# Forgetting attention in a hybrid decoder layer: who subtracts the weights' low parts, how two column minima are compared, and when two factor rows are fetched

## The chip, the cores and the metric

The kernel runs on one core of a Trainium2 chip. The metric is the device time of one launch in microseconds (us); of several runs the median is taken, and lower is better.

A core has five engines that work side by side, each with its own queue of instructions that it takes in order: TensorE (PE in the profile; its weight loads are listed apart as PEld), VectorE (DVE), ScalarE (ACT), GpSimd (POOL) and SyncE (SP, which here only issues DMAs). Engines wait for each other by semaphores.

## The reference

One decoder layer in fp32 over 1024 tokens of width 1024, cut here to what matters:

```python
h = rmsnorm(x, ln1)
ml_qk, ml_v, ml_o, ml_i, ml_f, fx_q, fx_k, fx_v, fx_f = split(h @ w_in)
# 4 mLSTM heads of 128, 8 forgetting heads of 64
mh = mlstm_chunkwise(mq, mk, mv, ig, lf)
mh = mh * rsqrt(mean(mh * mh, -1) + EPS) * ml_norm          # per token and head
ml_out = mh * sigmoid(ml_o)
s  = fq @ fk.T * 64**-0.5 + (c[q] - c[k])                   # c: running sum of log forget gates
p  = softmax(where(q >= k, s, -inf))
fx_out = p @ fv
x = x + concat([ml_out, fx_out]) @ w_out
x = x + cross_attention(rmsnorm(x, ln_x), rmsnorm(mem, ln_mem), w_xq, w_xkv, w_xo)   # 256 memory tokens
u = relu(rmsnorm(x, ln2) @ w_ff1)
out = rmsnorm(x + (u * u) @ w_ff2, ln_f)
```

## The kernel before

**Split products.** A fp32 product is made of three matmuls. Every operand is split into a high part (a copy rounded to the type fp32r) and a low part (the operand less its high part); lines 186, 187 and 188 multiply low by high, high by low and high by high into one PSUM bank. For weights, a DMA brings the raw tile (`wr`, 2 buffers), ACT writes the high part (`wh`, 3 buffers) and a subtraction gives the low part (`wl`, 3 buffers). Outside the stretch that the change concerns, this is `split` (lines 132 and 133, or 135 and 136 with a scale): ACT, then DVE.

**The order.** The kernel is written in a tile framework, which orders each engine's instructions from a timeline of its own. In regions marked `in_order()` the order on PE, ACT, DVE and POOL is the written one; the DMA queue of SP is still ordered by the framework.

**Closing an mLSTM head** (`ml_head`, from line 611). The factors of 1024 tokens stand in 8 columns of `fac`. `to_row` turns them into a row: 128x8 are transposed on PE, copied by ACT, stored by DMA to a row of `facd` in DRAM, and read back, broadcast to all 128 partitions, for the first half of the tokens (512). The second half is read by a DMA of its own (line 623). Each half is multiplied into the head's result (lines 626 and 627), split, and stored to `mix` in DRAM. Both rows use the buffer tag "a" (`r_a` in the trace), which has one buffer, so the second row's read waits until the first row has been used. The last head (`hd == MLH - 1`) is closed while the forgetting attention has begun.

**Forgetting attention.** For each of 8 heads, 8 row tiles of 128 queries: tile i sees the first (i + 1) x 128 keys, in one part (i < 4) or two. A `Tile` goes through `score` (two matmuls, lines 736 and 737, and a triangular mask, line 716), `top` (DVE's negated maximum of a part, line 743; after the second part the lower of the two columns, line 746), `exp` (ACT, line 749, with the sum along the row; line 751 for the correction between the parts) and `scale` (DVE's reciprocal, lines 756 and 757; POOL scales the weights, line 760). The columns (`c_mx`, `c_den`) have 3 buffers each. A `Values` step transposes 128 keys' weights of four tiles on PE (`turn`, line 775), splits them (`cut`: ACT line 132, DVE line 133, into `r_d` and `r_e`, or into one larger buffer in every third step) and multiplies by the values into bank `ov` (`add`, line 795). There is one `ov` bank: `fx_close` (ACT line 804, DVE line 805 into `r_f`) empties it before the next half head starts.

**Slots.** `slot()` runs one step of each in a fixed order: `fx_close` if a half head has ended, `turn`, the adds of two slots ago, `top`, `cut`, `exp`, `scale` of the slot before, the next score part, then filler, then one half of a weight split. 13 slots run scores alone first; then the product by `w_fv` (`token_major`, plain weight loads at line 174 and splits by `split`) stands between, in which the last mLSTM head is closed; then slots run with values. Per head there are 12 score parts and 12 value steps.

**Filler.** PE's spare time in the slots is filled with other products: the keys and values of cross attention (16 weight tiles of 1024 columns) and the first part of the output product (16 weight tiles of 640 columns, `out_unit`; results added at line 932). Each of these 32 weight tiles is loaded by `raw_load` (line 950) and split in two halves, one at the end of a slot, by `cut_half`:

```python
hi, lo = cuts_[sources[n][0]][-1]
c = slice(e * c // 2, (e + 1) * c // 2)
s.activation(hi[:, c], raw[:, c], AF.Copy)
(v if e else g).tensor_tensor(out=lo[:, c], in0=raw[:, c], in1=hi[:, c].bitcast(F32), op=ALU.subtract)
halves[0] += 1
if e:
    raw_load()
```

So POOL subtracts the first half (e = 0) and DVE the second; the load that follows a second half waits until the raw tile is free again.

Of the kernel before, what the change touches and what calls it, by code (L numbers as in the profile page):

```python
# [9 lines left out]
F32 = mybir.dt.float32  # L10
F32R = mybir.dt.float32r
AF = mybir.ActivationFunctionType
ALU = mybir.AluOpType
# [4 lines left out]
P = 128  # L18
T = 1024
TH = 512  # L20
# [3 lines left out]
MLH = 4  # L24
# [20 lines left out]
def hybrid_layer(ctx: ExitStack, tc: tile.TileContext, a: dict, out: bass.AP):  # L45
    nc = tc.nc
    v, s, g = nc.vector, nc.scalar, nc.gpsimd
# [11 lines left out]
    def sb(tag, shape, bufs, dt=F32):  # L59
        return pool.tile(shape, dt, tag=tag, name=name(tag), bufs=bufs)  # L60

    def act(dt=F32R):
        return sb("act", [P, 8, TH], 7, dt)
# [15 lines left out]
    def w2(tag, n=512, dt=F32, p=P):  # L79
        return sb("r_" + tag, [P, 512], BUFS[tag], dt)[:p, :n]  # L80

    def col(tag, n=1, bufs=3):
        return sb("c_" + tag, [P, 8], bufs)[:, :n]
# [6 lines left out]
    def sc():  # L90
        return ps_tile("sc")
# [4 lines left out]
    def ov_():  # L96
        return ps_tile("ov")
# [13 lines left out]
    load = nc.sync.dma_start  # L111
# [17 lines left out]
    def split(hi, lo, src, scale=None):  # L129

        if scale is None:
            s.activation(hi, src, AF.Copy)  # L132
            return v.tensor_tensor(out=lo, in0=src, in1=hi.bitcast(F32), op=ALU.subtract)  # L133
        else:
            s.activation(hi, src, AF.Copy, scale=scale)
            return v.scalar_tensor_tensor(out=lo, in0=src, scalar=scale, in1=hi.bitcast(F32), op0=ALU.mult, op1=ALU.subtract)
# [47 lines left out]
    def mm3(ps, w, x, first, last, more=False):  # L184

        nc.tensor.matmul(ps, w[1], x[0], start=first, stop=False, skip_group_check=more)  # L186
        nc.tensor.matmul(ps, w[0], x[1], start=False, stop=False, skip_group_check=more)  # L187
        nc.tensor.matmul(ps, w[0], x[0], start=False, stop=last, skip_group_check=more)  # L188

    def both(pair, f):  # L190
        return f(pair[0]), f(pair[1])
# [24 lines left out]
    def rsqrt_cols(*args):  # L216
        rsqrt_guess(*args)()
# [6 lines left out]
    def sum_cols(ps, src, n):  # L224
        for t in range(n):
            nc.tensor.matmul(ps[:, t : t + 1], src[:, t * P : (t + 1) * P], ones, start=True, stop=True)
# [21 lines left out]
    def to_row(dst, cols, n, at, bank=None):  # L248

        ps = (bank or ov_)()  # L250
        nc.tensor.transpose(ps[:n, :P], cols, ident)
        s.activation(dst[:n, :P], ps[:n, :P], AF.Copy)
        load(at.rearrange("o (t q) -> (o t) q", t=n), dst[:n, :P])
        w = min(dst.shape[1], n * P)
        return load(dst, at[:, :w].broadcast_to([P, w]))
# [14 lines left out]
    at = 0  # L270
# [39 lines left out]
    def mv_of(hd, t):  # L310

        return mv[hd // 2][:, t, hd % 2 * 256 : hd % 2 * 256 + 256]
# [15 lines left out]
    for k in range(KT):  # L328
        if k % 2 == 0:
            c = slice(k % 4 * 256, k % 4 * 256 + 512)  # L330
# [44 lines left out]
    z, e, q, lf = (small[:, i:j].rearrange("p (t c) -> p t c", c=c) for i, j, c in ((0, 128, GC), (128, 224, GW), (224, 320, GW), (320, 416, GW)))  # L375
# [188 lines left out]
    facd = dram.tile([MLH, T], F32, name="facd")  # L564

    def ml_head(hd, q, k, og, num1, den1):
        fac = col("fac", 8)
        nums = []
        dens = col("dens", 8)
        sqs = col("sqs", 8)  # L570
        for hf in range(2):
            nmb = w2("a")
            load(nmb, rows[hd : hd + 1, hf * TH : hf * TH + TH].broadcast_to([P, TH]))
            num = ov_()
            acc = den1 if hf else w2("b")
            last = 4 * hf + 3
            for j in range(4 * hf, last + 1):
                d0 = j - 4 * hf
                c0 = min(d0 * P, 256)
                sp = sc()  # L580
                ks = both(k, lambda z: z[:, j * P : (j + 1) * P])
                mm3(sp[:, c0:], ks, both(q, lambda z: z[:, hf * TH + c0 : hf * TH + TH]), True, True)
                wt = acc if j == 0 else w2("c")
                s.activation(wt[:, c0:], nmb[:, c0:], AF.Exp, bias=gcol[:, j, hd : hd + 1])
                n_ = d0 * P + P - c0
                g.affine_select(out=wt[:, c0 : c0 + n_], in_=wt[:, c0 : c0 + n_], pattern=[[1, n_]], compare_op=ALU.is_ge, fill=0.0, base=c0 - d0 * P, channel_multiplier=-1)
                v.scalar_tensor_tensor(out=wt[:, c0:], in0=sp[:, c0:], scalar=float(P) ** -0.5, in1=wt[:, c0:], op0=ALU.mult, op1=ALU.mult)
                wh, wl = w2("d", dt=F32R), w2("e", dt=F32R)
                split(wh[:, c0:], wl[:, c0:], wt[:, c0:])
                if j:  # L590
                    g.tensor_tensor(out=acc[:, c0:], in0=wt[:, c0:], in1=acc[:, c0:], op=ALU.add)
                vj = mv_of(hd, j)
                mm3(num[:, c0:], (vj[:, :P], vj[:, P:]), (wh[:, c0:], wl[:, c0:]), d0 == 0, j == last)
            sq = w2("c")
            if hf:
                nsb = num1
                v.tensor_tensor(out=nsb, in0=num, in1=nsb, op=ALU.add)
                s.activation(sq, nsb, AF.Square)
            else:
                nsb = w2("f")  # L600
                s.activation(nsb, num, AF.Copy)
                s.activation(sq, num, AF.Square)
            ps = sc()
            sum_cols(ps[:, 0:4], acc, 4)
            sum_cols(ps[:, 4:8], sq, 4)
            s.activation(dens[:, 4 * hf : 4 * hf + 4], ps[:, 0:4], AF.Abs)
            v.tensor_copy(sqs[:, 4 * hf : 4 * hf + 4], ps[:, 4:8])
            nums.append(nsb)
        v.tensor_tensor(out=dens, in0=dens, in1=emc[:, :, hd], op=ALU.max)
        rd = col("rd", 8)  # L610
        v.reciprocal(rd, dens)
        v.tensor_tensor(out=sqs, in0=sqs, in1=rd, op=ALU.mult)
        v.tensor_tensor(out=sqs, in0=sqs, in1=rd, op=ALU.mult)
        rsqrt_cols(fac, sqs, 1.0 / P, 8)
        v.tensor_tensor(out=fac, in0=fac, in1=rd, op=ALU.mult)
        yield
        for hf in range(2):
            fb = w2("a")
            at = facd[hd : hd + 1]
            if hf == 0:  # L620
                to_row(fb, fac, 8, at, sc)
            else:
                load(fb, at[:, TH:].broadcast_to([P, TH]))
            yield
            y = nums[hf]
            v.scalar_tensor_tensor(out=y, in0=y, scalar=vec[:, VEC["ml_norm"] + hd : VEC["ml_norm"] + hd + 1], in1=fb, op0=ALU.mult, op1=ALU.mult)
            v.scalar_tensor_tensor(out=y, in0=og[:, hf * TH : hf * TH + TH], scalar=1.0, in1=y, op0=ALU.add, op1=ALU.mult)
            yh, yl = w2("y", dt=F32R), y.bitcast(F32R)
            split(yh, yl, y, 0.5)
            load(mix[hf, 0, :, hd], yh.bitcast(F32))  # L630
            load(mix[hf, 1, :, hd], yl.bitcast(F32))
# [86 lines left out]
    class Tile:  # L718
# [23 lines left out]
        def top(self, e):  # L742
            v.tensor_reduce(out=self.mxs[:, e : e + 1], in_=self.ps[e], axis=mybir.AxisListType.X, op=ALU.max, negate=True)
            if e:

                v.tensor_tensor(out=self.mxs[:, 1:2], in0=self.mxs[:, 0:1], in1=self.mxs[:, 1:2], op=ALU.min)

        def exp(self, e):
            s.activation(self.pt[:, slice(*self.parts[e])], self.ps[e], AF.Exp, bias=self.mxs[:, e : e + 1], accum_out=self.dens[:, e : e + 1])
# [195 lines left out]
    def raw_load():  # L945
        n = len(raws_)
        if n < len(sources):
            src = sources[n][1]
            raw = sb("wr", [P, 1024], 2)[:, : src.shape[-1]]
            last_raw[:] = [load(raw, src)]  # L950
            raws_.append(raw)

    def cut_half():

        n, e = divmod(halves[0], 2)
        raw = raws_[n]
        c = raw.shape[-1]
        if e == 0:
            cuts_.setdefault(sources[n][0], []).append(tuple(sb(t, [P, 1024], 3, F32R)[:, :c] for t in ("wh", "wl")))
        hi, lo = cuts_[sources[n][0]][-1]  # L960
        c = slice(e * c // 2, (e + 1) * c // 2)
        s.activation(hi[:, c], raw[:, c], AF.Copy)
        (v if e else g).tensor_tensor(out=lo[:, c], in0=raw[:, c], in1=hi[:, c].bitcast(F32), op=ALU.subtract)
        halves[0] += 1
        if e:
            raw_load()

    def cut_for(u, most=99):

        while most and halves[0] < 2 * len(sources) and sources[halves[0] // 2][0] <= u:  # L970
            cut_half()
            most -= 1
# [97 lines left out]
    for step in fill:  # L1070
        n, e = divmod(halves[0], 2)
# [8 lines left out]
    for hf in range(2):  # L1080
        hi, lo = act(), act()
# [623 lines left out]
```

## Time and profile before

| | before |
|---|---|
| median of 3 runs | 1520.9 us (1520.22 to 1521.38) |
| span of the profiled execution | 1518.6 us |
| that execution's own device time | not recorded apart from its span |
| granted TensorE clock, mean | 0.997 |
| PE idle in the span | 1518.6 - 1498.9 = 19.7 us |
| HBM traffic | 195 GB/s over the span |

The span runs from the first to the last instruction of one profiled execution; the device time of a run includes what lies around it. Busy times are per engine and overlap. A line number in the trace is that of the kernel before; `r_a` to `r_y` are buffers of the tags "a" to "y", `c_` are columns, `tp`, `sc`, `mm` and `ov` PSUM banks, `wr`, `wh` and `wl` the raw, high and low weights. The trace shows the work that is changed between about 370 and 590 us of the span.

### The profile page before, as it was taken

How to read it: one execution, taken by the hardware profiler on the slowest of the kernel's cores; microseconds unless marked ns; L12 is line 12 of the kernel's file. 1: busy time of each engine (PE TensorE's matmuls, PEld its weight loads, DVE VectorE, ACT ScalarE, POOL GpSimd, SP SyncE). 2: the span in 40 equal slices, each digit the busy share in tenths (PEclk: the TensorE clock that was granted, in tenths of full speed). 3: DMA queues.
4: the chain of work that ended last, by engine and by line, in shares of the span. 5: the costliest groups of instructions: out<-in, count | busy, mean ns of one | idle time of the engine just before them, and what ended most of it. 6: DMA issues, size and time to landing. Idle time of an engine off the chain costs nothing.

```text
span 1518.6 us, 21919 instructions
## 1 busy us (share of the span) xinstructions
PE 1498.9 (99%) x7697; PEld 1260.1 (83%) x7697; DVE 1100.2 (72%) x1744; ACT 723.7 (48%) x1349; POOL 436.9 (29%) x497
## 2 busy tenths in 40 slices
PE   8999999999999999999999999999999999999997
PEld 8988888889898888788888888888888888888887
DVE  7676675765798875854457887887887788777765
ACT  7333343334688763644343456565556332222124
POOL 1003030413455441001100033343344644333312
PEclk9999999999999999999999999999999999999998
DMA  6332333446887958953334436876775966555623
GB/s 240 89 107 87 113 104 127 131 130 164 267 252 225 291 195 281 321 195 119 122 135 155 164 123 232 281 276 239 271 256 217 360 260 222 222 222 215 255 85 111
DMA packets 118673, 298.28 MB, mean 196 GB/s; under 512 B 13202, under 2 KB 27852, under 8 KB 112420
## 3 DMA queue, kind: packets, MB, share of 16 engines
q1 hardware_dynamic: 118276, 296.79, 57.1%
q8 instruction: 60, 0.98, 0.3%
q14 instruction: 49, 0.40, 0.1%
q10 hardware_dynamic: 288, 0.11, 0.1%
HBM read 200.13 MB, written 96.72 MB: 195 GB/s over the span
## 4 chain that ended last, share of the span: by engine, by line
PE 92%; DMA 3%; DVE 2%; issue 1%; ACT 1%; POOLq 0%; SPq 0%; POOL 0%; DVEq 0%; ACTq 0%
PE tp L186 8%; PE tp L188 8%; PE tp L187 8%; PE sc L186 6%; PE sc L188 6%; PE sc L187 6%; PE m L186 6%; PE m L187 6%; PE m L188 6%; PE mm L186 6%; PE mm L187 6%; PE mm L188 6%; PE ov L186 2%; PE ov L187 2%; PE ov L188 2%; PE ov L795 2%
## 5 line engine op out<-in xcount | busy, mean ns | idle before, releaser
L186 PE MATMUL tp<-act,wl 128*128 128x512 f32 (+1 forms) x456 | 178.6, 392 | 0.0
L187 PE MATMUL tp<-act,wh 128*128 128x512 f32 (+1 forms) x456 | 178.5, 392 | 0.0
L188 PE MATMUL tp<-act,wh 128*128 128x512 f32 (+1 forms) x456 | 178.5, 392 | 0.0
L132 ACT ACTIVATE wh<-wr 128x1024 fp32r<-128x1024 f32 (+3 forms) x100 | 96.0, 961 | 116.4 <-PE tp L188 37.2
L133 DVE TENSOR_TENSOR wl<-wr,wh 128x1024 fp32r<-128x1024 f32 (+3 forms) x100 | 116.7, 1168 | 17.4 <-ACT wh L132 16.9
L186 PE MATMUL mm<-act,wl 128*128 128x512 f32 (+1 forms) x328 | 126.0, 384 | 0.5 <-DVE r_d L1091 0.5
L187 PE MATMUL mm<-act,wh 128*128 128x512 f32 (+1 forms) x328 | 125.8, 384 | 0.0
L188 PE MATMUL mm<-act,wh 128*128 128x512 f32 (+1 forms) x328 | 125.5, 383 | 0.0
L186 PE MATMUL m<-act,wl 128*128 128x512 f32 (+1 forms) x312 | 119.2, 382 | 0.8 <-DVE r_d L1091 0.8
L188 PE MATMUL m<-act,wh 128*128 128x512 f32 (+1 forms) x312 | 119.1, 382 | 0.0
L187 PE MATMUL m<-act,wh 128*128 128x512 f32 (+1 forms) x312 | 119.1, 382 | 0.0
L188 PEld LDWEIGHTS tp<-act,wh 128*128 128x128 f32 x456 | 85.7, 188 | 19.6
L186 PEld LDWEIGHTS tp<-act,wl 128*128 128x128 f32 x456 | 85.7, 188 | 19.1
L187 PEld LDWEIGHTS tp<-act,wh 128*128 128x128 f32 x456 | 85.8, 188 | 18.9
L186 PE MATMUL sc<-act,wl 128*128 128x512 f32 (+1 forms) x260 | 100.7, 387 | 0.0
L187 PE MATMUL sc<-act,wh 128*128 128x512 f32 (+1 forms) x260 | 100.5, 386 | 0.0
L188 PE MATMUL sc<-act,wh 128*128 128x512 f32 (+1 forms) x260 | 100.5, 386 | 0.0
L1439 POOL TENSOR_TENSOR z<-wr 128x256 f32<-128x256 f32 x56 | 52.7, 963 | 146.9 <-DMA wr<-w_ff2q 129.8
L132 ACT ACTIVATE w<-wr 128x768 fp32r<-128x768 f32 (+2 forms) x31 | 25.5, 825 | 131.2 <-PE tp L188 69.1
L132 ACT ACTIVATE wh<-z 128x1024 fp32r<-128x1024 f32 (+2 forms) x55 | 52.5, 956 | 65.0 <-POOL z L1439 29.8
L133 DVE TENSOR_TENSOR wl<-z,wh 128x1024 fp32r<-128x1024 f32 (+2 forms) x55 | 66.0, 1200 | 9.1 <-ACT wh L132 9.1
L188 PEld LDWEIGHTS mm<-act,wh 128*128 128x128 f32 x328 | 61.6, 188 | 12.9 <-issue 0.2
(656 smaller groups left out, 4189.6 us busy)
## 6 DMA issues: line engine op xcount, KB each, us to landing
act<-right SPq DMA_DIRECT2D x35, 1024.0 KB
right<-r_d SPq DMA_DIRECT2D x70, 256.0 KB
right<-w SPq DMA_DIRECT2D x56, 256.0 KB
wr<-w_ff2q SPq DMA_DIRECT2D x28, 512.0 KB
act<-fqk SPq DMA_DIRECT2D x48, 256.0 KB
wr<-w_in SPq DMA_DIRECT2D x20, 512.0 KB
wr<-w_ff SPq DMA_DIRECT2D x20, 512.0 KB
fqk<-r_p SPq DMA_DIRECT2D x32, 256.0 KB
```

What stands on the lines that cost most here:

```text
L132: s.activation(hi, src, AF.Copy)
L133: return v.tensor_tensor(out=lo, in0=src, in1=hi.bitcast(F32), op=ALU.subtract)
L186: nc.tensor.matmul(ps, w[1], x[0], start=first, stop=False, skip_group_check=more)
L187: nc.tensor.matmul(ps, w[0], x[1], start=False, stop=False, skip_group_check=more)
L188: nc.tensor.matmul(ps, w[0], x[0], start=False, stop=last, skip_group_check=more)
L795: nc.tensor.matmul(self.ov[:, c0:], self.fv[:, self.j], t[:, c0:], start=self.j == 0 and t is self.p[1], stop=self.last and t is self.p[0])
L1439: g.tensor_tensor(out=o, in0=x, in1=y, op=op)
```

## The change

Three edits. In `cut_half` the second half's subtraction is given to GpSimd as the first is. In `top` the lower of the two columns is found by an operation of one tensor with a per-partition scalar instead of one of two tensors. In `ml_head`, for the last head alone, the two rows get two buffers, "a" and "d"; both reads are issued right behind `to_row`'s store, and the high part of the second half's result goes to a buffer "e" instead of "y". For the other three heads the loads stay where they were (`hf != end` is true for `hf = 1` alone, and for the last head for `hf = 0` alone). Behind line 616 the new kernel's lines have numbers higher by 2. The numbers of instructions on each engine are unchanged but for the 32 subtractions that pass from DVE to POOL.

```diff
@@ ml_head
         yield
+        end = hd == MLH - 1
+        fbs = [w2("a"), w2("d")] if end else [None, None]
+        at = facd[hd : hd + 1]
         for hf in range(2):
-            fb = w2("a")
-            at = facd[hd : hd + 1]
+            fb = fbs[hf] or w2("a")
             if hf == 0:
                 to_row(fb, fac, 8, at, sc)
-            else:
-                load(fb, at[:, TH:].broadcast_to([P, TH]))
+            if hf != end:
+                load(fbs[1] or fb, at[:, TH:].broadcast_to([P, TH]))
             yield
...
-            yh, yl = w2("y", dt=F32R), y.bitcast(F32R)
+            yh, yl = w2("e" if end and hf else "y", dt=F32R), y.bitcast(F32R)
             split(yh, yl, y, 0.5)
@@ Tile.top
-                v.tensor_tensor(out=self.mxs[:, 1:2], in0=self.mxs[:, 0:1], in1=self.mxs[:, 1:2], op=ALU.min)
+                v.tensor_scalar(out=self.mxs[:, 1:2], in0=self.mxs[:, 1:2], scalar1=self.mxs[:, 0:1], scalar2=None, op0=ALU.min)
@@ cut_half
-        (v if e else g).tensor_tensor(out=lo[:, c], in0=raw[:, c], in1=hi[:, c].bitcast(F32), op=ALU.subtract)
+        g.tensor_tensor(out=lo[:, c], in0=raw[:, c], in1=hi[:, c].bitcast(F32), op=ALU.subtract)
```

## The prediction, made before the changed kernel was run

> **What bounds the kernel now.** I read the page first. TensorE (PE) is busy for almost the whole span:
>
> ```profile
> span 1518.6 us, 21919 instructions
> PE 1498.9 (99%) x7697; PEld 1260.1 (83%) x7697; DVE 1100.2 (72%) x1744; ACT 723.7 (48%) x1349; POOL 436.9 (29%) x497
> ```
>
> The timed runs have their median at 1520.9 us, 2.3 us above the span of the profiled execution; what lies around the span is not shown by itself, so I make the sum on the span and add it to the median as it stands. The runs lie between 1520.22 and 1521.38, and about 0.2% (3.0 us) is what a measurement of this kernel can tell from no change.
>
> All three edits act between 360 and 600 us, so next I asked for the busy times of that stretch alone:
>
> ```profile
> 360.00:600.00 240.00, 236.53 (x1587) 211.90 (x1586) 187.91 (x443) 163.16 (x438) 103.53 (x161) 1.00 0.79 246
> ```
>
> The columns after the length are PE, weight load, VectorE (DVE), ScalarE (ACT) and GpSimd (POOL). PE stands still for 240.00 - 236.53 = 3.47 us, and the clock is 1.00. So nothing that speeds another engine can return much more than these 3.47 us, while work made late can cost without such a ceiling. DVE, at 78%, is the busiest engine beside PE, POOL the idlest at 43%: the change moves work from the one to the other. The question is which of the 3.47 us of waits end on DVE.
>
> **The moved subtraction.** The groups of this stretch, kept apart by shape, give its price on either engine, and the price of the comparison (line 746):
>
> ```profile
> L963 POOL TENSOR_TENSOR wl<-wr,wh 128x512 fp32r<-128x512 f32 x16 | 21.4, 1340 | 5.1 <-ACT wh L962 3.8 <-issue 1.3
> ...
> L963 DVE TENSOR_TENSOR wl<-wr,wh 128x512 fp32r<-128x512 f32 x16 | 14.8, 923 | 1.2 <-ACT wh L962 1.1
> ...
> L963 POOL TENSOR_TENSOR wl<-wr,wh 128x320 fp32r<-128x320 f32 x16 | 14.0, 876 | 26.9 <-ACT wh L962 21.6 <-DVE r_p L932 2.7 <-DVE r_b L932 2.6
> ...
> L963 DVE TENSOR_TENSOR wl<-wr,wh 128x320 fp32r<-128x320 f32 x16 | 10.1, 631 | 1.1 <-ACT wh L962 1.0
> ...
> L746 DVE TENSOR_TENSOR c_mx<-c_mx 128x1 f32<-128x1 f32 x32 | 8.9, 279 | 1.1
> ```
>
> 32 second halves leave DVE: 14.8 + 10.1 = 24.9 us. POOL takes on 16 of 1.34 us and 16 of 0.876 us, 35.5 us at most. POOL goes to about 103.5 + 35.5 = 139 of 240 us (58%), DVE to about 163 (68%). Both have room on average. PE's matmuls are the same ones, so its own work does not change.
>
> Does DVE's relief reach PE? Here is the worst place, from the timeline of POOL, ACT, DVE and PE (start, length, engine, line, and in brackets the idle time before it):
>
> ```profile
> 489.59 1.45 POOL L963 TENSOR_TENSOR wl<-wr,wh 128x512 fp32r<-128x512 f32 x1
> ...
> 489.73 0.48 ACT L132 ACTIVATE r_d<-tp 128x384 fp32r<-128x384 f32 x1
> ...
> 489.86 1.73 DVE L963 TENSOR_TENSOR wl<-wr,wh 128x512 fp32r<-128x512 f32 x1
> ...
> 490.58 0.60 ACT L804 ACTIVATE r_c<-ov 64x512 f32<-64x512 f32 x1
> ...
> 491.56 0.28 PE L188 MATMUL mm<-wh,act 128*128 128x256 f32 x1
> ...
> 491.85 0.54 DVE L133 TENSOR_TENSOR r_e<-tp,r_d 128x384 fp32r<-128x384 f32 x1
> ...
> 492.45 0.33 PE L775 MATMUL tp<-ident,w 128*128 128x128 f32 x1 [0.61 <-DVE r_e L133]
> ...
> 492.75 0.69 DVE L805 TENSOR_TENSOR r_f<-ov,r_c 64x512 f32<-64x512 f32 x1
> ...
> 493.49 0.50 PE L795 MATMUL ov<-r_e,w 128*128 128x512 f32 x1 [0.66 <-DVE r_f L805]
> ```
>
> The reader is to see a DVE subtraction of 1.73 us that begins inside POOL's and ends after it. Behind it in DVE's queue stand the split of the transposed weights (491.85) and the sum that frees the output bank (492.75), and PE waits for both, 0.61 + 0.66 = 1.27 us. Without it the split has its input at 489.73 + 0.48 = 490.21 and the sum has its own at 490.58 + 0.60 = 491.18, each more than a microsecond before it now starts. Both waits should go. ACT's inputs are late next, and they are early enough for PE.
>
> A second such place, at the change from one head to the next:
>
> ```profile
> 426.53 0.59 ACT L804 ACTIVATE r_c<-ov 64x512 f32<-64x512 f32 x1
> ...
> 426.54 1.15 DVE L963 TENSOR_TENSOR wl<-wr,wh 128x512 fp32r<-128x512 f32 x1
> ...
> 427.72 0.68 DVE L805 TENSOR_TENSOR r_f<-ov,r_c 64x512 f32<-64x512 f32 x1
> ...
> 428.46 0.50 PE L795 MATMUL ov<-r_e,w 128*128 128x512 f32 x1 [0.44 <-DVE r_f L805]
> ```
>
> The sum could start when ACT is done, at 426.53 + 0.59 = 427.12 instead of 427.72. That is 0.60 us, more than the 0.44 us waited.
>
> **What holds POOL's added work.** Where POOL waits now, and what waits for the halves:
>
> ```profile
> POOL act L760 <- DVE c_den L757: 44.5, 22, 7.5
> ...
> POOL w L760 <- DVE c_den L757: 18.8, 14, 4.3
> ...
> SPq L950 <- DVE wl L963: 22.9, 14, 4.5
> ...
> ACT wh L962 <- DMA wr<-w_xv: 1.9, 1, 1.9
> ```
>
> POOL's scalings of the softmax weights (line 760) wait 44.5 + 18.8 = 63.3 us for DVE's reciprocals. A second half that runs in such a gap delays no scaling, and the 35.5 us would fit in it 1.8 times. Queued behind a second half on POOL are the next slot's scalings, for which ACT's exponentials and DVE's maxima wait three tiles later, through their three column buffers, and PE's transposes. Its own reader is PE's filler matmul. One of the tightest second halves:
>
> ```profile
> 407.77 0.68 DVE L963 TENSOR_TENSOR wl<-wr,wh 128x512 fp32r<-128x512 f32 x1
> ...
> 410.71 0.28 PE L187 MATMUL mm<-wl,act 128*128 128x256 f32 x1
> ```
>
> It ends 2.26 us before its use; 1.34 instead of 0.68 us takes 0.66 us of that, and a scaling ahead of it less than 1.6 more. This still fits, barely.
>
> The load of the next weights (line 950) stands on SP's queue behind the second half: 14 such waits now, 22.9 us. It is issued later by the same 0.66 us or more, and the loads of queries and keys behind it too. In the order of the changed program one to three of those loads have moved ahead of it at several places. ACT has waited for weight data for 1.9 us only, at one place, so mostly nothing is lost. I price this from 0 to 1.0 us (half of that 1.9 us once more) and take 0.4, nearer to no wait.
>
> **The comparison.** In the queries of lines 746 and 757 (lengths: least, median, most) and in the timeline:
>
> ```profile
> L746 DVE TENSOR_TENSOR c_mx<-c_mx x32: 151/160/1073, 375.8 to 558.3; 128x1 f32<-128x1 f32 x32
> ```
>
> ```profile
> L757 DVE RECIPROCAL c_den<-c_den x64: 144/156/167, 371.6 to 562.3; 128x1 f32<-128x1 f32 x64
> ```
>
> ```profile
> 400.96 1.30 POOL L963 TENSOR_TENSOR wl<-wr,wh 128x512 fp32r<-128x512 f32 x1
> ...
> 401.21 1.07 DVE L746 TENSOR_TENSOR c_mx<-c_mx 128x1 f32<-128x1 f32 x1
> ```
>
> A comparison of one column takes 1.07 us when it falls into a POOL subtraction, and ends with it (402.28 against 402.26). A reciprocal of one column, with one tensor input, has never taken over 0.167 us. The row that the new form resembles most is the reciprocal, since it reads one tensor and a scalar: 8.9 - 32 x 0.156 = 3.9 us of DVE time freed at best, nothing at worst. No PE wait above ends on line 746, so it adds nothing to the sum and only shortens DVE's queue.
>
> [...]
>
> **The two factor rows.** In the chain of waits, and then in the timeline:
>
> ```profile
> 373.10 4.12 DMA r_a<-facd
> ...
> 378.02 3.87 DMA r_a<-facd
> ```
>
> ```profile
> 381.92 0.75 DVE L626 SCALAR_TENSOR_TENSOR r_f<-r_f,vec,r_a 128x512 f32<-128x512 f32 x1 [2.00 <-DMA r_a<-facd]
> ...
> 382.77 0.47 ACT L749 ACTIVATE act<-sc,c_mx 128x256 f32<-128x256 f32 x1 [2.03 <-DVE c_mx L746]
> ...
> 383.39 0.50 PE L736 MATMUL sc<-act 128*128 128x512 f32 x1 [0.41 <-ACT act L749]
> ```
>
> The second row is fetched only after the first has been used, DVE waits 2.00 us for it with a comparison queued behind, ACT's exponential waits for that, and PE 0.41 us. With a buffer of its own the second load is issued right behind the first, near 373.5, and lands near 378. The three links shorten and the 0.41 us go. The other moved pieces (the two stores of the results and the five filler matmuls that now stand behind the row's transpose) have no reader close by: nothing. The borrowed buffers are needed again only at the first value tiles.
>
> **What stays.** Two waits at the change to the slots end on ACT's own order:
>
> ```profile
> 395.20 0.45 PE L736 MATMUL sc<-act 128*128 128x384 f32 x1 [0.72 <-ACT act L749]
> ...
> 399.01 0.38 PE L736 MATMUL sc<-act 128*128 128x256 f32 x1 [0.37 <-ACT w L749]
> ```
>
> The order of these instructions on ACT and PE is not changed, so 1.09 us remain.
>
> **Sum.** 1.27 + 0.44 + 0.41 = 2.12 us go by the bracketed idle times. They count short: between the starts at 491.56 and 492.45 lie 0.89 us, of which 0.28 count as busy, although such matmuls otherwise follow each other faster. With at most 0.2 us more for each of four waits the gain is between 2.1 and 2.9 us; I take 2.6. Less 0.4 for the later loads: 2.2 us. The span becomes 1516.4, the time 1520.9 - 2.2 = 1518.7 us.
>
> **Rivals.**
> (a) *All waits go.* A shorter DVE queue also removes the 1.09 us at the change and the rest: 3.47 + 6 x 0.2 = 4.7 us at most, 1516.5 us taken. For it: DVE is at 78%, and 29 us of its 188 may go. Against: those waits end on ACT. Chance 0.22; were the new comparison held up as the old one is, I would give it 0.12.
> (b) *It does nothing that shows.* PE has 99%, and ACT, at 163 of 240 us, takes DVE's place at the same points: only the row's 0.41 us are left, 1520.5 us. Against: both ACT inputs above are ready long before. Chance 0.15.
> (c) *POOL falls behind.* At each head's change tiles come one per slot instead of one per two, and POOL has a scaling and a subtraction in each. If a whole subtraction is late there, three tiles later maxima and exponentials wait and PE with them: 1.34 us in four of eight heads and 0.876 in four, 8.9 us, 1529 us with DVE's gain just lost; 1525 us if it is half of the heads. It decides when the gaps per head, 63.3 / 8 = 7.9 us, fall below the added 35.5 / 8 = 4.4 us. Against: they are nearly twice as long, but they are a mean. Chance 0.18.
>
> **Numbers.** Forecast 0.45, 1518.7 us; a third of it (0.15) lies beyond a gain of 3.0 us. Faster by over 0.2%: 0.22 + 0.15 = 0.37. Within 0.2%: 0.30 + 0.15 = 0.45. Slower: 0.18. The range takes in (a) down to 1515.5 and the better part of (c) up to 1524.0.
>
> **What would show it.** Right: the second halves on POOL at 1.3 and 0.88 us; line 746's successor at 0.15 to 0.2 us throughout; no PE wait on DVE's r_f or r_e at the two places; one landing before both row multiplications; PE idle of about 1.3 us between 360 and 600. Wrong: PE, ACT or DVE waiting for POOL's line 760 successor; ACT waiting several times for weight data; PE idle above 3.5 us in that stretch; or a difference outside of it.

## Result and the profile after

The changed kernel has a median of 1525.7 us (6 runs, 1523.26 to 1530.04), the kernel before 1521.43 us (6 runs, 1520.22 to 1522.96). The ratio is 1.0029, with a 95% interval of 1.0019 to 1.0039: 4.4 us slower, where 2.2 us faster was forecast, and beyond the 1524.0 us at which the forecast's range ended. The runs also lie further apart than before, 6.8 us against 2.7. The profiled execution is the mildest of the six (span 1521.5 us, as in the run of 1523.26), so it shows 2.9 us of the loss.

The page of the changed kernel, and its stretch from 360 to 600 us (PE, weight load, DVE, ACT, POOL, then the clock):

```profile
span 1521.5 us, 21865 instructions
...
PE 1498.9 (99%) x7697; PEld 1260.5 (83%) x7697; DVE 1081.7 (71%) x1712; ACT 723.1 (48%) x1349; POOL 467.1 (31%) x529
```

```profile
360.00:600.00 240.00, 233.47 (x1568) 209.72 (x1567) 164.69 (x409) 161.66 (x437) 134.28 (x193) 0.99 0.76 241
```

PE stands still for 6.53 us there, 3.06 more than before. That the spans differ by nearly as much is chance, for a slower clock, shown below, comes on top of the standing still. Both traces hold the same 7697 matmuls in the same order, so their starts can be set side by side: up to 360 us the changed kernel is ahead by 0.24 us, and the product with `z` that starts at 600.57 us before starts at 604.52 us. The stretch is 4.2 us longer, and 1.0 us comes back behind it, which nothing here explains. DVE and POOL moved as foreseen (164.7 and 134.3 us busy), and PE waits in no place for POOL.

Its groups of moved and changed instructions, and the query of the new comparison (least, median, most):

```profile
L965 POOL TENSOR_TENSOR wl<-wr,wh 128x512 fp32r<-128x512 f32 x32 | 41.4, 1298 | 10.5 <-ACT wh L964 9.0 <-issue 1.1 <-POOL act L762 0.5
L965 POOL TENSOR_TENSOR wl<-wr,wh 128x320 fp32r<-128x320 f32 x32 | 28.2, 889 | 22.3 <-ACT wh L964 21.0 <-DMA mix<-r_y 0.7 <-issue 0.7
```

```profile
L748 DVE TENSOR_SCALAR c_mx<-c_mx x32: 204/214/216, 374.9 to 562.2; 128x1 f32<-128x1 f32 x32
```

The prices of the subtraction were right. The comparison no longer stretches: it has a most of 0.216 us, though its usual length has grown from 0.160 to 0.214 us.

What is new stands in the waits of the changed kernel in this stretch (total, times, longest). Before, ACT waited for weights of the slots once, 1.9 us, and PE for ACT's exponentials for 1.1 us:

```profile
PE sc L738 <- ACT act L751: 4.2, 3, 2.0
ACT wh L964 <- DMA wr<-w_xv: 4.1, 1, 4.1
...
ACT wh L964 <- DMA wr<-w_xk: 2.7, 2, 2.5
...
PE ov L797 <- DVE r_f L807: 1.6, 2, 0.8
...
ACT wh L964 <- DMA wr<-w_out_a: 1.0, 1, 1.0
```

ACT waits for raw weights, its exponentials stand behind that wait in its queue, and PE's next scores need the banks that these read. Here is the dearest place, first before, then after, from the timelines of SP, ACT and PE:

```profile
451.91 0.32 SPq L861 DMA_DIRECT2D z<-mix  x1
452.33 0.37 SPq L950 DMA_DIRECT2D wr<-w_xv  x1
453.16 0.32 SPq L861 DMA_DIRECT2D z<-mix  x1
...
456.37 0.63 ACT L962 ACTIVATE wh<-wr 128x512 fp32r<-128x512 f32 x1 [1.91 <-DMA wr<-w_xv]
```

```profile
452.91 1.57 SPq L863 DMA_DIRECT2D z<-mix  x2
454.57 0.38 SPq L952 DMA_DIRECT2D wr<-w_xv  x1
...
458.63 0.63 ACT L964 ACTIVATE wh<-wr 128x512 fp32r<-128x512 f32 x1 [4.06 <-DMA wr<-w_xv]
...
460.25 0.50 PE L738 MATMUL sc<-act 128*128 128x512 f32 x1 [2.00 <-ACT act L751]
```

Before, the weight load goes out between two loads of `z` (a tile of head results for the output product; the first product with such a tile starts at 513.6 us). After, both loads of `z` stand ahead of it, and each waits until the results that it reads have been stored to `mix` (SP waits 2.9 and 0.9 us for these stores). And behind the stall the clock falls to 0.59 in a row of 4 us (the column before the last two):

```profile
456.00:460.00 4.00, 2.25 (x16) 1.77 (x14) 0.23 (x1) 1.37 (x4) 0.93 (x2) 1.00 0.76 284
460.00:464.00 4.00, 3.75 (x14) 3.32 (x15) 3.68 (x10) 3.44 (x13) 3.01 (x4) 0.59 0.31 87
464.00:468.00 4.00, 4.00 (x34) 3.92 (x33) 1.96 (x8) 2.73 (x7) 2.43 (x5) 0.98 0.86 259
```

The missing clock is 4 x 0.41 + 4 x 0.02 = 1.7 us, so 3.4 us at half speed; rows of 0.5 us show 0.50 from 461.0 to 464.0 us. A second place is near 408 us, where a load of `x`, whose sum comes some 120 us later, stands ahead of the weights and waits for its buffer (3.8 us, for a store of `r_b`):

```profile
404.21 0.34 SPq L926 DMA_DIRECT2D r_b<-x  x1
...
408.51 0.63 ACT L964 ACTIVATE wh<-wr 128x512 fp32r<-128x512 f32 x1 [2.47 <-DMA wr<-w_xk]
...
410.14 0.50 PE L738 MATMUL sc<-act 128*128 128x512 f32 x1 [1.48 <-ACT act L751]
```

That load of `x` stood ahead of the weights before too, but there it went out at 402.01, earlier than the raw tile was free, and the weights followed at 403.60 without ACT having to wait.

A third place is near 521 us, where before had no wait. ACT is late by its wait for `w_out_a`, so it empties the output bank late, and PE waits for DVE's sum behind that:

```profile
519.58 0.47 ACT L964 ACTIVATE wh<-wr 128x320 fp32r<-128x320 f32 x1 [0.96 <-DMA wr<-w_out_a]
520.08 0.60 ACT L806 ACTIVATE r_c<-ov 64x512 f32<-64x512 f32 x1
...
521.44 0.51 PE L797 MATMUL ov<-r_e,w 128*128 128x512 f32 x1 [0.81 <-DVE r_f L807]
```

Its weight load goes out at 514.59: POOL has ended the second half that frees the raw tile at 513.42, and three loads of queries and keys now stand ahead of it. Before, it went out at 509.79, ahead of those loads.

### The profile page after: what moved, and what is told of

Same layout as the page of the kernel before. It is cut to its first block, busy times and chain, and to the rows that moved or that the text cites. A ratio compares the mean times of both kernels' runs of the same rounds, so it can differ in the third digit from the quotient of the medians.

```text
span 1521.5 us, 21865 instructions
## 1 busy us (share of the span) xinstructions
PE 1498.9 (99%) x7697; PEld 1260.5 (83%) x7697; DVE 1081.7 (71%) x1712; ACT 723.1 (48%) x1349; POOL 467.1 (31%) x529
## 4 chain that ended last, share of the span: by engine, by line
PE 90%; DMA 4%; DVE 2%; ACT 2%; issue 1%; POOL 0%; SPq 0%; POOLq 0%; DVEq 0%; ACTq 0%
PE tp L186 8%; PE tp L188 8%; PE tp L187 8%; PE sc L186 6%; PE sc L188 6%; PE sc L187 6%; PE mm L186 6%; PE mm L187 6%; PE mm L188 6%; PE m L186 6%; PE m L188 6%; PE m L187 6%; PE ov L186 2%; PE ov L187 2%; PE ov L188 2%; PE ov L797 2%
## 5 line engine op out<-in xcount | busy, mean ns | idle before, releaser
L965 POOL TENSOR_TENSOR wl<-wr,wh 128x512 fp32r<-128x512 f32 (+1 forms) x64 | 69.6, 1093 | 32.8 <-ACT wh L964 29.9
```

What stands on the lines that cost most here:

```text
L965: g.tensor_tensor(out=lo[:, c], in0=raw[:, c], in1=hi[:, c].bitcast(F32), op=ALU.subtract)
```

## Experiments

The theories. **L**: weight loads come late, ACT waits, PE waits. In the form **L1** because GpSimd ends the second half later and so frees the raw tile later; in the form **L2** because of what stands ahead of the load on SP's queue. **R**: the row loads push other loads back. **C**: the new comparison is on the path. **B**: GpSimd's subtractions hold DVE's two-input instructions (the old comparison took up to 1.07 us beside one). **V**: DVE is the scarce engine.

| kernel | median us (runs) | before us (runs) | ratio, 95% interval |
|---|---|---|---|
| changed | 1525.7 (6) | 1521.43 (6) | 1.0029, 1.0019 to 1.0039 |
| e1 halves alone | 1528.77 (5) | 1523.13 (27) | 1.0040, 1.0028 to 1.0053 |
| e2 rows alone | 1521.33 (11) | 1523.13 (27) | 0.9993, 0.9984 to 1.0002 |
| e3 comparison alone | 1522.79 (11) | 1523.13 (27) | 0.9999, 0.9991 to 1.0008 |
| e4 rows and comparison | 1520.72 (11) | 1523.13 (27) | 0.9989, 0.9980 to 0.9998 |
| e5 changed, loads ordered | 1521.5 (11) | 1521.64 (33) | 0.9995, 0.9985 to 1.0004 |
| e6 before, loads ordered | 1520.74 (11) | 1521.64 (33) | 0.9992, 0.9984 to 1.0001 |
| e7 rows, comparison, loads ordered | 1521.55 (11) | 1521.64 (33) | 0.9992, 0.9983 to 1.0001 |
| e8 both halves on DVE | 1526.13 (11) | 1521.64 (33) | 1.0024, 1.0015 to 1.0034 |
| e9 before, one load exchanged | 1521.85 (12) | 1521.07 (35) | 1.0007, 0.9996 to 1.0018 |
| e10 halves, loads ordered | 1521.93 (11) | 1521.07 (35) | 1.0004, 0.9996 to 1.0013 |
| e11 both on DVE, loads ordered | 1522.32 (11) | 1521.07 (35) | 1.0005, 0.9997 to 1.0014 |
| e12 as e7, two halves on GpSimd | 1519.01 (11) | 1521.07 (35) | 0.9984, 0.9976 to 0.9993 |
| e13 changed, z's loads ordered | 1524.67 (11) | 1522.34 (17) | 1.0014, 1.0004 to 1.0023 |
| e14 changed, x's loads ordered | 1528.6 (6) | 1522.34 (17) | 1.0038, 1.0026 to 1.0051 |

**One edit at a time.** e1 has only `(v if e else g)` turned into `g`; e2 only the hunk of `ml_head`; e3 only the new comparison; e4 the two without the first.

> The first edit alone: GpSimd subtracts both halves; the old comparison and the old row loads. Theory L (late loads): the raw tile is released later and its next load stands behind other loads on SP's queue, so ScalarE waits for weights, and TensorE for scores behind it. Then this kernel carries the whole loss: 4 to 6 us above the kernel before, with ScalarE waiting for wr two to four times (6 us or more in all) and TensorE stalls of over 1 us near 408 and 458 us. Theory R (rows): the loss near 408 us comes from the row loads; then this kernel is only 2 to 3 us slower and TensorE does not stall near 408 us. Theory C (comparison): the loss is that of the new comparison; then this kernel is within 1 us of before or faster.

> The third edit alone: both factor rows of the last mLSTM head are read at once. Theory L: 0.4 to 1 us faster than before, the stall of 0.41 us at 383 us gone, none above 0.6 us near 408 us. Theory R: the value stores land later, the load of x ahead of the weights is held by them, and TensorE stalls by 1 us or more near 408 us: 1 to 2 us slower than before. Theory C: as theory L.

> The second edit alone: the comparison of one tensor with a scalar column. Theories L and R: within 0.7 us of before; the new form takes about 0.21 us each time (32 times 0.21 = 6.8 us of VectorE instead of 8.9). Theory C: the 0.05 us more in the typical case stand on the way from maxima to exponentials, 32 times: 0.8 to 1.7 us slower.

> The change without its first edit: rows at once and the new comparison; VectorE keeps the second halves. Theory L: 0.4 to 1.2 us faster than before, ScalarE waits for weights once (1.9 us) as before. Theory R: 1 to 2 us slower. Theory C: 0.4 to 1.3 us slower.

The first edit carries the loss: 6.1 us by the ratio, though its interval overlaps that of the whole change. R and C fall: rows and comparison cost nothing, and together are 1.7 us faster. e1's order of SP shows what has happened: with the second subtractions on POOL, the framework's timeline has set both loads of `z` ahead of the weights, which none of e2 to e4 does. From e1's timelines:

```profile
456.78 1.57 SPq L861 DMA_DIRECT2D z<-mix  x2
458.45 0.38 SPq L950 DMA_DIRECT2D wr<-w_xv  x1
...
462.45 0.63 ACT L962 ACTIVATE wh<-wr 128x512 fp32r<-128x512 f32 x1 [6.80 <-DMA wr<-w_xv]
...
464.07 0.79 PE L736 MATMUL sc<-act 128*128 128x512 f32 x1 [4.73 <-ACT act L749]
```

But e2, whose order there is that of before, has a stall of 2.24 us at the same place in its profile, with 4.33 us of wait: the first `z` load went out 6.7 us after the store that it waits for was issued (447.27 to 453.98), 4.7 us in the profile of before (447.17 to 451.91). So the place was at its edge already, and in these two profiles the landing of a store makes the difference.

**The order of loads.** e5 is the changed kernel with `z`'s and `x`'s loads issued behind named weight loads; e6, e7, e10 and e11 have the same edit:

```diff
+raw_ins = []                       # raw_load() appends its load
 def mix_tile(k, hf):
...
+        with tc.issue_after(raw_ins[8 + 4 * hf].ins):
             load(t[:, p_].bitcast(F32), mix[hf, p_, :, k])
...
-load(x, a["x"][:, n, hf * TH : hf * TH + TH])
+with tc.issue_after(raw_ins[10 + 8 * hf + n].ins):
+    load(x, a["x"][:, n, hf * TH : hf * TH + TH])
```

> The changed kernel, with the loads of z from mix and of x told to be issued behind named weight loads on SP's queue, so that they cannot stand ahead of the next weight load; nothing else. Theory L2 (the weight loads are late because of what stands ahead of them on SP's queue): the wait of ScalarE for w_xv near 458 us goes from 4.1 to under 2 us, TensorE's stall of 2.15 us there and the half clock behind it (1.4 us) go, and part of the 1.64 us near 408 us: 3 to 5 us faster than the changed kernel, so within 1 us of the kernel before. Theory L1 (late because GpSimd finishes the second half later): the waits stay, no more than 1 us is won. Theory B (GpSimd's subtractions hold VectorE's two-input instructions): no more than 1 us is won either, and the stalls near 495 and 520 us are the larger part of what is left.

> The kernel before with the same order of loads on SP. Theory L2: the kernel before has the same weakness at 457 us with less of it (ScalarE waits 1.9 us there in its profile, 2.2 to 4.3 us in those of the rows and of the comparison): 0.3 to 1.5 us faster than before, and the times lie closer together. Theories L1 and B: no difference over 0.3 us.

> Rows at once, the new comparison, second halves on VectorE, and the same order of loads on SP: the parts that did not lose. Theory L2: 1.7 us less than before (as the rows and the comparison together gave) and 0.3 to 1.0 us more from the order: 2 to 2.7 us faster than before. Theories L1 and B: 1.4 to 2 us faster, as without the order.

> The first edit alone (both halves on GpSimd), with z's and x's loads behind named weight loads. Theory L2: the 5.6 us that this edit alone cost go but for 0 to 1.5 us. Theory L1: 3 us or more stay. Theory B: 4 us or more stay.

e5 is level with before, and e10 nearly: 5.5 of e1's 6.1 us go without one subtraction moved back. That is L2, and against L1 and B, which wanted most of it to stay. e6 and e7 came out equal, 1.2 us faster by a ratio whose interval just reaches 1: the 0.3 to 1.5 us for e6 fit, e7's 2 to 2.7 us do not, so the 1.7 us of e4 do not add to the order's gain. In e5's timelines:

```profile
450.55 0.33 SPq L956 DMA_DIRECT2D wr<-w_xv  x1
...
456.03 0.63 ACT L969 ACTIVATE wh<-wr 128x512 fp32r<-128x512 f32 x1 [2.50 <-DMA wr<-w_xv]
...
457.66 0.50 PE L738 MATMUL sc<-act 128*128 128x512 f32 x1 [0.43 <-ACT act L751]
...
483.06 0.33 SPq L956 DMA_DIRECT2D wr<-w_xk  x1
...
488.69 0.63 ACT L969 ACTIVATE wh<-wr 128x512 fp32r<-128x512 f32 x1 [2.47 <-DMA wr<-w_xk]
...
490.53 0.44 PE L738 MATMUL sc<-act 128*128 128x384 f32 x1 [1.58 <-ACT act L751]
```

The load at 450.55 still takes over 5 us to be of use. The one at 483.06 goes out as POOL ends the second half that frees its buffer (two halves from 480.48, 2.55 us long, to 483.03); in e7's trace DVE has done that at 481.81. So L1 exists too, at this place, and costs PE 1.58 us there. e5 is rid of the loss, but the gain of 2.6 us that was forecast before the term for the loads does not show in it either. The place near 521 us is still there (ACT waits 1.00 us for `w_out_a`, PE 0.86 us), so PE waits for 0.43 + 1.58 + 0.86 = 2.9 us behind late weights. A wait of PE for `r_f` there is in the profile of every kernel whose second halves are all on POOL (0.81 to 1.33 us: the changed kernel, e1, e5, e10, e13, e14) and, of the others, in those of e8 and e11 alone, which have both halves on DVE (0.47 and 0.49 us). How much of it is POOL's later end and how much the loads of queries and keys was not tested.

e9 makes only the exchange, in the kernel before:

```diff
-last_raw[:] = [load(raw, src)]
+if n == 10:                        # the load of w_xv near 452 us
+    early_z[1] = mix_tile(MLH, 1)  # both loads of z first
+    with tc.issue_after(early_z[1][1].ins):
+        last_raw[:] = [load(raw, src)]
```

> The kernel before, with one exchange on SP's queue and nothing else: the load of w_xv near 452 us stands behind the second load of z from mix, as it does in the changed kernel, instead of between the two. Theory L2: it is issued about 1.25 us later, ScalarE waits over 3 us instead of 1.9, TensorE loses the excess over 1.9 us there, and where that stall passes 2 us the clock halves for some 3 us (1.4 us more): 1.2 to 3.5 us slower than before. Theories L1 and B, in which the place of GpSimd's subtraction is needed for the loss: within 0.5 us of before.

```profile
451.62 1.58 SPq L865 DMA_DIRECT2D z<-mix  x2
453.31 0.37 SPq L961 DMA_DIRECT2D wr<-w_xv  x1
...
457.49 0.63 ACT L975 ACTIVATE wh<-wr 128x512 fp32r<-128x512 f32 x1 [3.36 <-DMA wr<-w_xv]
...
459.11 0.50 PE L736 MATMUL sc<-act 128*128 128x512 f32 x1 [1.28 <-ACT act L749]
```

In the trace it does what L2 says, without any GpSimd subtraction moved. In the times it is 1.1 us, at the foot of what was expected, with an interval that reaches no difference. So one exchange alone is, by the middle of its interval, a quarter of the loss, and the times alone do not prove it. The next two divide the order in the changed kernel.

> The changed kernel with z's loads from mix alone put behind named weight loads; x's loads stay where they are. If the place at 458 us carries the loss: 2.5 to 4 us faster than the changed kernel (2.15 us of stall and 1.4 us of half clock), so 0 to 1.5 us above before, and the stall of 1.6 us near 408 us stays. If the place near 408 us carries it: under 1.5 us faster than the changed kernel.

> The changed kernel with x's loads alone put behind named weight loads; z's loads stay. If the place at 458 us carries the loss: 0.5 to 1.5 us faster than the changed kernel, so 2.5 to 4 us above before, with the stall of over 2 us near 458 us and the half clock behind it still there. If the place near 408 us carries it: 2.5 us or more faster than the changed kernel.

With `z` ordered and `x` not, the ratio falls from 1.0029 to 1.0014; with `x` ordered and `z` not, it is 1.0038, not told from 1.0029. Both are needed to come back to 1.0, and `z` is the larger part: between e14 and e5 lie 0.43%, between e13 and e5 0.19%. The sizes were missed: e13 lies 2.1 us above before instead of 0 to 1.5, e14 5.8 us instead of 2.5 to 4. (In e13's profile PE loses a further 1.16 and 1.79 us near 627 and 631 us, outside the stretch, which no theory here covers.) PE's rows of e13 (near 408 us) and of e14 (near 458 us), with the stretch behind each:

```profile
411.82 0.50 PE L738 MATMUL sc<-act 128*128 128x512 f32 x1 [1.88 <-ACT act L751]
```

```profile
412.00:414.00 2.00, 2.00 (x15) 1.87 (x16) 1.71 (x6) 1.96 (x6) 1.32 (x2) 1.00 0.24 98
```

```profile
462.37 0.80 PE L738 MATMUL sc<-act 128*128 128x512 f32 x1 [5.15 <-ACT act L751]
```

```profile
462.00:464.00 2.00, 1.63 (x5) 1.45 (x6) 1.71 (x5) 2.00 (x7) 1.33 (x2) 0.50 0.05 18
```

Set side by side, the place at 458 us follows one rule in these kernels: PE's wait is ACT's wait for `w_xv` less 2.1 us (in e8, which is not in the table, 3.31 and 1.08 us). Near 408 us it is ACT's wait less 1.0 us: 2.47 and 1.48 us in the changed kernel, 2.88 and 1.88 us in e13.

| kernel | load issued at us | ACT waits us | PE waits us | lowest clock of the 4 us rows behind |
|---|---|---|---|---|
| before | 452.33 | 1.91 | 0 | 1.00 |
| e5 | 450.55 | 2.50 | 0.43 | 1.00 |
| e3 | 453.35 | 2.66 | 0.57 | 1.00 |
| e9 | 453.31 | 3.36 | 1.28 | 1.00 |
| e12 | 450.82 | 3.57 | 1.48 | 1.00 |
| changed | 454.57 | 4.06 | 2.00 | 0.59 |
| e2 | 454.40 | 4.33 | 2.24 | 0.60 |
| e1 | 458.45 | 6.80 | 4.73 | 0.57 |
| e14 | 456.57 | 7.24 | 5.15 | 0.52 |

**VectorE and GpSimd.** e8 is before with `v` for both halves, e11 that with the loads ordered, e12 is e7 with two second halves on GpSimd:

```diff
-(v if e else g).tensor_tensor(out=lo[:, c], ...
+(v if e and n not in (5, 15) else g).tensor_tensor(out=lo[:, c], ...
```

> The kernel before with both halves of the low parts on VectorE, so that GpSimd subtracts nothing and cannot hold VectorE; the order on SP changes with it at several places. Theory B: the waits near 491 to 493 us (1.27 us) shrink, no split of 128x256 takes over 0.5 us, and it is 0 to 1.5 us faster though VectorE gets 25 us more to do. Theory V (VectorE is the scarce engine, as the prediction had it): 2 to 6 us slower, with TensorE waiting for r_e, r_f and the scores.

> Both halves on VectorE, with z's and x's loads behind named weight loads. Theory L2: the kernel with both halves on VectorE was slow for its order of loads too, so this one is within 1 us of before. Theory V (VectorE is the scarce engine): it stays 2 to 4 us slower than before.

> Rows at once, the new comparison, the order of loads, and of the 32 second halves only two on GpSimd: that of the weight tile before the stall at 428 us and that of the tile before the two stalls at 491 to 493 us, the two places that the prediction took its gain from. If the prediction's terms hold: 1.5 to 2.2 us faster than the same kernel without the two (which was within the noise 0.1 us from the kernel before on its median, 0.08% faster in the fast runs), about 1518.5 to 1519.5 us beside 1521 of before. If ScalarE's inputs take VectorE's place there: no difference.

e8 was slower by 3.7 us, as V had it, but e11 is within 0.8 us of before: most of e8's loss was again its order of loads, and V falls as the larger part. B's forecast of a gain fails too, but its mechanism is in e8's stretch and group:

```profile
360.00:600.00 240.00, 234.37 (x1577) 209.95 (x1576) 190.42 (x474) 162.04 (x437) 72.69 (x129) 1.00 0.79 244
```

```profile
L963 DVE TENSOR_TENSOR wl<-wr,wh 128x512 fp32r<-128x512 f32 x32 | 22.5, 705 | 3.8 <-ACT wh L962 3.7
```

DVE does all 64 subtractions and is busy for only 2.5 us more than with 32 of them (190.42 against 187.91), since one now takes 705 instead of 923 ns, one of 128x320 498 instead of 631 ns, and a comparison 181 instead of 279 ns on the mean: POOL's subtractions had held DVE's subtractions and comparisons by these amounts. In e1, where POOL does all 64, a comparison takes 417 ns.

e12 is the fastest: 0.16% (0.07 to 0.24%) below before, 2.4 us. Beside e7, the same kernel without the two halves, it is 0.08% or 1.2 us faster with intervals that overlap, so the 1.5 to 2.2 us that were expected of the two places are not shown as a time. Their waits show them. PE's first products behind the two places of the prediction:

```profile
426.84 0.50 PE L797 MATMUL ov<-r_e,w 128*128 128x512 f32 x1
...
491.77 0.50 PE L797 MATMUL ov<-r_e,w 128*128 128x512 f32 x1
```

Neither has an idle time in front any more (0.44 us and 0.66 us before; 0.45 and 0.66 us in e7).

## Why the prediction was wrong

**The waits on DVE: right for the two places, not for what all 32 halves do.** The two places that end on DVE's queue behave as worked out in e12, where two halves are moved. In the changed kernel the first is gone too, and the second has come back in another form, one that the prediction did not see: two subtractions in a row on POOL hold a split of 128x256 for 1.32 us (the three others of `r_p` take 0.41 to 0.59 us), and the sum stands behind it.

```profile
492.71 2.72 POOL L965 TENSOR_TENSOR wl<-wr,wh 128x512 fp32r<-128x512 f32 x2
492.95 1.32 DVE L133 TENSOR_TENSOR r_p<-r_p 128x256 fp32r<-128x256 f32 x1 [0.46 <-ACT r_p L132]
...
496.41 0.50 PE L797 MATMUL ov<-r_e,w 128*128 128x512 f32 x1 [0.79 <-DVE r_f L807]
```

So of the 2.6 us some 0.8 us came back here, and as much again near 521 us, there by a late load.

**The row loads: right in the trace.** Both reads go out together (372.64 and 373.01), the second multiplication starts 1.28 us behind the first (379.05 against 377.77), and PE's wait of 0.41 us at 383 us is gone. As a time it is not told from none (e2).

**The comparison: not held up, and as a gain in time nothing.** Of the 3.9 us of DVE's time 2.1 us came (8.9 to 32 x 0.214 = 6.8), for the new form takes 0.214 us and not the 0.156 us of the reciprocal. The other end of the prediction's estimate, a new form held up like the old one, is not shown: its longest is 0.216 us, in a stretch in which POOL subtracts for 69.6 us, where the old form went up to 1.07 us in the kernel before.

**The loads: the step that failed.** The prediction priced the later weight loads "from 0 to 1.0 us" and took 0.4, by ACT's one wait of 1.9 us. Three things were wrong in that term. It took ACT's wait of 1.9 us at no cost to PE for a sign of room, when the table shows that the room is 2.1 us in all and was used up (near 408 us it is 1.0 us): each further microsecond is one of PE. It looked for the delay in POOL's 0.66 us, while most came from SP's queue, where it had counted the query and key loads that had moved ahead but not those of `z`, which had moved ahead too, and of `x`, which stood there already; these wait themselves. And it left out the clock, which was 0.50 for some 3.4 us behind the stall of 2.00 us. In the profiled execution the two places cost 2.00 + 1.48 us of wait and 1.7 us of clock, against 0.4, and the place near 521 us 0.81 us more. By the runs, the order of loads is worth 5 to 5.5 us (e1 against e10, and the changed kernel against e5). With that order mended the term is still not 0.4: the 2.9 us that PE waits behind late weights in e5 are as much as the 2.6 us of gain, and e5 is level with before.

**The rivals.** (c) gave nearly the time that was measured, 1525 us, by a mechanism that did not happen, so its nearness is luck: PE and DVE wait nowhere in the stretch for POOL's scalings, ACT once, 0.5 us. (a) and (b) did not come either.

**What the profile says and what it is.** The chain of waits of the changed kernel puts the late load down to POOL:

```profile
453.49 1.08 POOL wl L965
454.57 4.03 DMA wr<-w_xv
```

That is the subtraction of another tile's half, which happened to end there. e13 and e9 decide it: in e13 POOL subtracts just the same, and ACT waits 1.95 us and PE not at all; in e9 the load is late without POOL. What stays open: why the changed kernel's runs spread over 6.8 us. The loads of `z` that go out 4.7 to 7.8 us after the store that they wait for (profiles of before and of e14), together with the half clock, could do it, but only one execution of each kernel has a trace.

## What to carry to other kernels

Before moving work between engines, list every DMA that is issued after it or passes it on the queue, and ask of each what it waits for: here two prefetches for a product some 60 us later, put ahead of an urgent load, held it while they waited themselves (it went out at 454.57 instead of 452.33 us). An engine that waits 1.9 us at no cost to the bound engine is no proof of slack (here the bound engine noticed from 2.1 us on); look how much later the bound engine would notice. And where a scheduler writes the order of the DMA queue from its own timeline, pin the urgent loads first, then judge the edit: here the same edit went from 0.40% slower to level.

## What was not expected of the hardware

The clock. In the stretch from 360 to 600 us of these traces a PE stall of 1.88 us (e13) or less left it at 1.00. Behind the stall of 2.00 us (changed) rows of 0.5 us show 0.50, behind those of 2.24 us (e2) and 4.73 us (e1) rows of 4 us show 0.60 and 0.57, and at the end of the 5.15 us of e14 a row of 2 us shows 0.50. In the 4 us rows from 456 to 468 us the missing clock adds up to 1.7 us in the first three, which is 3.4 us at half speed, and to twice that in e14. These are numbers of this stretch: at the start of the kernel before, PE's first matmul comes at 6.42 us, and the rows around it show 1.00.

One column compared with a scalar took 0.214 us and never more than 0.216 us (changed kernel); with two tensors it took 0.160 us and up to 1.07 us (before). And in this kernel the subtractions that POOL does beside DVE cost DVE much of what they save it: taking the other 32 back, DVE was busy for 2.5 us more, not for the 19 us that they take in e8 (16 of 0.705 and 16 of 0.498 us).
